# Token norm with tokens on partitions, a small weight piece asked earlier, and a first row in four blocks

## The chip, the cores and the metric

The kernel runs on one core of a Trainium2 chip. A core has five engines that run side by side, each through its own list of instructions: TensorE (PE, matrix products, with its weight loads shown apart as PEld), VectorE (DVE), ScalarE (ACT), GpSimd (POOL) and SyncE (SP, which here only asks for transfers). They wait for one another by semaphores. Data comes from memory through 16 DMA engines. The metric is the device time of one execution in microseconds, lower is better.

## The reference

One block of a diffusion backbone, for 512 latent tokens of 2048 channels and 256 context tokens. What matters for this case is the head of it: each token is divided by the root of the mean of its squares, multiplied by a per-channel gain, and shifted; gain and shift come from a product of the conditioning vectors with a weight matrix (the modulation).

```
shift, scale, gate = split(silu(c) @ w_ada + b_ada, 3)
shift_c, scale_c, gate_c = split(silu(c_ctx) @ w_ada + b_ada, 3)
rms(v) = v * rsqrt(mean(v * v, axis=-1) + EPS) * norm_g
h  = rms(x)   * (1 + scale)   + shift       # 512 x 2048
hc = rms(ctx) * (1 + scale_c) + shift_c
p  = h @ w_in                               # q, k, v, gates, Fourier branch: 2048 x 9216
...                                         # attention, Fourier mixing, projections
out = rms_final(x + gate * y)
```

## The kernel before

All large products are made in three terms of a high and a low part (`mm3`, lines 339 to 341: high by high, high by low, low by high), with both parts of f32r type. A weight piece of 128 x 1024 that arrives as f32 is split by `split_from`: ACT copies it to the high part (line 181), DVE subtracts that for the low part (line 182).

The channels lie on partitions: `xt` holds x transposed, 16 rows (`kb`, the kernel's word for a block of 128 channels) of 128 partitions by 512 tokens. The first stage, before the kernel's long steady part, does this:

- SP asks for x in nine transfers (line 477, tile `xt`), then for the weights of the first rows' modulation (tile `wa`, `in_w_ss`; the first matrix, `kb` = 0, in one half and two quarters, which are its second half) and for pieces of the input projection (tile `wr`, `in_w_start`, line 217). All these go through one queue in the order of the program.
- `token_norms` squares x (ACT, for two rows DVE), adds the squares of two rows (DVE, line 546) and sums them over the 128 partitions by products with ones on PE (line 548), eight groups, one after each pair. Between groups PE gets a product that nobody reads (`warm`, line 528) to keep it busy. Then ACT takes the root (line 553), DVE the reciprocal (line 554), and `spread` (line 560) puts the 512 values on all partitions, in a PSUM tile `pc`.
- `matvec(0, 0)` and `matvec(0, 1)` (line 567) multiply the conditioning vectors by the two halves of the first modulation matrix, with `spread` between them in PE's order. `taken` (line 583) copies the result to the tile `ado`, `turned` transposes it (line 588), `factors` makes gain and shift from it (lines 599 to 602).
- The first row: `by_root` (line 614) multiplies x by the reciprocal root from PSUM, `row_hi` (line 618, ACT) applies gain and shift and rounds to the high part, `scaled` and `row_lo` (lines 621 and 625, DVE) make the low part. `start_work` then runs the products of that row with the first pieces: 256 columns (lines 680, 681, 687), then the other 768 (`mm3`).

In this stage PE, ACT and DVE run in the order in which the program was written (`manual_schedule`). PE therefore waits in line: what stands behind a waiting product waits too.

## Time and profile before

| what | us |
|---|---|
| median of 3 runs | 1287.12 (1286.21 to 1287.29) |
| the profiled execution, device time | 1286.97 |
| its span, first to last instruction | 1285.2 |
| PE busy | 1269.6 (99%) |
| PE weight loads busy | 1045.2 (81%) |
| DVE busy | 991.0 (77%) |
| ACT busy | 683.2 (53%) |
| POOL busy | 173.2 (13%) |

The device time holds the span and 1.77 us around it. The busy time of PE is modelled from pipelined products, so its share says that PE has work nearly all the time, not that it runs at its peak. In rows of a timeline, a group of alike instructions is merged to one row with its count; an f32 product that is one instruction in the program's order is two in the trace.

### The profile page before, as it was taken

To read this page: it belongs to the slowest core of one execution; us is meant where nothing else is said; L and a number is where in the kernel's file an instruction comes from. 1 tells how busy PE (TensorE), PEld (TensorE's weight loads), DVE (VectorE), ACT (ScalarE), POOL (GpSimd) and SP (SyncE) were. 2 spreads that over 40 slices of the span, in tenths; PEclk is the share of its full clock that TensorE was granted. 3 is DMA by queue.
4 is the path that set the end of the run, shared out by engine and by line. 5 is a ranking of instruction groups with operands and counts; after the bars stand their busy time and mean duration, and the time that the engine had idled before them with its cause. 6 is when DMAs were issued, how large, how long until landed. Compare 5 with 4: busy or idle time off the path is not lost.

```text
span 1285.2 us, 17638 instructions
## 1 busy us (share of the span) xinstructions
PE 1269.6 (99%) x6562; PEld 1045.2 (81%) x6562; DVE 991.0 (77%) x1305; ACT 683.2 (53%) x1077; POOL 173.2 (13%) x226
## 2 busy tenths in 40 slices
PE   8999999999999999999999999999999999999997
PEld 5677888888888888888888888888888888888886
DVE  5767899889778787748687756778898777787677
ACT  5322765555466564543355445766667646465544
POOL 0000121111102011012021011011100221211310
PEclk9999999999999999999999999999999999999999
DMA  9998798888898998887879897578852989998986
GB/s 378 412 368 344 242 204 254 229 240 239 234 315 209 320 271 254 291 197 188 282 204 288 254 259 234 180 234 250 265 178 67 260 241 258 245 207 222 227 207 179
DMA packets 104343, 319.07 MB, mean 248 GB/s; under 512 B 9889, under 2 KB 32801, under 8 KB 100289
## 3 DMA queue, kind: packets, MB, share of 16 engines
q1 hardware_dynamic: 54336, 195.24, 41.8%
q0 software_dynamic: 27600, 100.29, 37.0%
q10 hardware_dynamic: 22320, 22.42, 5.1%
q8 instruction: 51, 0.84, 0.3%
q14 instruction: 36, 0.29, 0.1%
HBM read 283.30 MB, written 34.61 MB: 247 GB/s over the span
## 4 chain that ended last, share of the span: by engine, by line
PE 82%; DVE 3%; DMA 2%; ACT 2%; issue 1%; SPq 0%; ACTq 0%
PE banks L339 10%; PE banks L340 10%; PE banks L341 10%; PE x L341 9%; PE x L339 9%; PE x L340 9%; PE y L341 8%; PE y L340 8%; PE y L339 8%; PE banks L1551 2%; DMA wr<-in_w_pab 1%; DVE wlo L182 1%; DMA s<-yb_d 1%; PE banks L1665 1%; DVE s L182 0%
## 5 line engine op out<-in xcount | busy, mean ns | idle before, releaser
L181 ACT ACTIVATE whi<-R 128x1024 fp32r<-128x1024 f32 x138 | 145.1, 1058 | 143.7 <-PE banks L341 47.5
L182 DVE TENSOR_TENSOR wlo<-R,whi 128x1024 fp32r<-128x1024 f32 x138 | 167.7, 1221 | 61.2 <-ACT whi L181 60.9
L182 DVE TENSOR_TENSOR wlo<-wr,whi 128x1024 fp32r<-128x1024 f32 (+1 forms) x122 | 147.3, 1213 | 62.7 <-ACT whi L181 62.5
L181 ACT ACTIVATE whi<-wr 128x1024 fp32r<-128x1024 f32 (+1 forms) x122 | 127.4, 1050 | 123.4 <-PE y L341 33.0
L339 PE MATMUL banks<-whi,s 128*128 128x512 f32 (+1 forms) x400 | 157.8, 394 | 0.9 <-ACT ev L1160 0.7
L340 PE MATMUL banks<-wlo,s 128*128 128x512 f32 (+1 forms) x400 | 155.9, 390 | 0.0
L341 PE MATMUL banks<-whi,s 128*128 128x512 f32 (+1 forms) x400 | 155.8, 389 | 0.0
L339 PE MATMUL x<-whi,s 128*128 128x512 f32 x352 | 137.1, 390 | 0.0
L341 PE MATMUL x<-whi,s 128*128 128x512 f32 x352 | 137.0, 389 | 0.0
L340 PE MATMUL x<-wlo,s 128*128 128x512 f32 x352 | 136.9, 389 | 0.0
L292 POOL DMA_DIRECT2D R<-in_w_g x68 | 59.5, 874 | 484.7 <-DVE wlo L182 290.2
L340 PE MATMUL y<-wlo,s 128*128 128x512 f32 x316 | 123.0, 389 | 0.1
L339 PE MATMUL y<-whi,s 128*128 128x512 f32 x316 | 122.9, 389 | 0.0
L341 PE MATMUL y<-whi,s 128*128 128x512 f32 x316 | 122.8, 389 | 0.0
L181 ACT ACTIVATE s<-wr 128x512 fp32r<-128x512 f32 (+2 forms) x93 | 60.8, 677 | 66.0 <-DMA wr<-cf_d 24.4
L182 DVE TENSOR_TENSOR s<-wr,s 128x512 fp32r<-128x512 f32 (+2 forms) x93 | 66.7, 749 | 31.8 <-ACT s L181 30.9
L339 PEld LDWEIGHTS banks<-whi,s 128*128 128x128 f32 x400 | 75.2, 188 | 16.6 <-ACT ev L1160 1.1
L341 PEld LDWEIGHTS banks<-whi,s 128*128 128x128 f32 x400 | 75.2, 188 | 15.3
L340 PEld LDWEIGHTS banks<-wlo,s 128*128 128x128 f32 x400 | 75.2, 188 | 13.9 <-DVE wlo L182 0.2
L340 PEld LDWEIGHTS x<-wlo,s 128*128 128x128 f32 x352 | 66.1, 188 | 13.8
L341 PEld LDWEIGHTS x<-whi,s 128*128 128x128 f32 x352 | 66.1, 188 | 13.7
L339 PEld LDWEIGHTS x<-whi,s 128*128 128x128 f32 x352 | 66.1, 188 | 13.6
(333 smaller groups left out, 2794.0 us busy)
## 6 DMA issues: line engine op xcount, KB each, us to landing
wr<-in_w_g SPq DMA_DIRECT2D x124, 512.0 KB, 5.6
R<-in_w_g POOLq DMA_DIRECT2D x68, 512.0 KB, 7.4
wa<-in_w_ss SPq DMA_DIRECT2D x31, 1024.0 KB, 9.5
R<-in_w_g SPq DMA_DIRECT2D x32, 512.0 KB, 5.8
wr<-in_w_gate SPq DMA_DIRECT2D x32, 512.0 KB, 5.1
wr<-in_w_o SPq DMA_DIRECT2D x24, 512.0 KB, 7.1
R<-in_w_o POOLq DMA_DIRECT2D x24, 512.0 KB, 8.9
wr<-in_w_pab SPq DMA_DIRECT2D x20, 512.0 KB, 6.1
```

The lines of the kernel that those rows point to most:

```text
L181: first = nc.scalar.activation(hi, src, ACT.Copy)
L182: return first, nc.vector.tensor_tensor(lo, src, hi.bitcast(F32), op=ALU.subtract)
L292: chained[:] = [nc.gpsimd.dma_start(chain[e.pc], e.nxt, accum_op=ALU.add)]
L339: nc.tensor.matmul(o, ah, bh, start=start, stop=False, skip_group_check=cont)
L340: nc.tensor.matmul(o, ah, bl, start=False, stop=False, skip_group_check=cont)
L341: nc.tensor.matmul(o, al, bh, start=False, stop=stop, skip_group_check=cont)
L1551: nc.tensor.transpose(tp[:, k * P : (k + 1) * P], p[:, k * P : (k + 1) * P], ident)
L1665: last_turn[0] = nc.tensor.transpose(tp[:, k // 2, 256 * (k % 2) + P * t : 256 * (k % 2) + P * t + P], m[:, t, k * P : k * P + P], ident)
```

## The change

Three parts, all in the first stage.

1. The sums of squares. Before, ones (32 columns wide) were PE's weights and the squares streamed through, so that each group of 128 tokens had its sums along the free axis, in a strip of 32 partitions of its own. Now the squares of 128 tokens are the weights and one column of ones streams, so that the sums stand with tokens on partitions, in four columns. The last pair of rows isn't added by DVE any more; both rows go to PE. Root and reciprocal work on 128 x 4 instead of 128 x 128. `spread` uses a column of the reciprocals, repeated 128 times, as weights and the identity as the streaming side. The selection table `pick`, and its memsets on POOL, are gone. One `warm` product instead of three follows the first transpose.
2. The small piece `wr` of 128 x 256 is asked for ahead of the last quarter of the first modulation matrix instead of behind it.
3. `row_hi` and `row_lo` of the first row go in four blocks of 128 tokens. And `by_root(0)` stands ahead of the copy of the spread roots to SBUF (`rx`), on which it does not depend.

```
@@ wada_load @@
             for k in (0, 4) if (kb, h) == (0, 1) else (0,):
                 n = 4 if (kb, h) == (0, 1) else 8
+                if (kb, h, k) == (0, 1, 4):
+                    load_start()
                 ask(nc.sync, r[-1][:, k : k + n, :], w_ss[kb, :, 8 * h + k : 8 * h + k + n, :])
...
     wada = {0: wada_load(0)}
-    for _ in range(2):
-        load_start()
+    load_start()
@@ token_norms @@
-        t = hm_tile([P, 2, T], F32, name=uid("nm"))
-        pick, r = t[:, 0, :].rearrange("p (t c) -> p t c", t=4), t[:, 1, :P]
-        nc.gpsimd.memset(pick, 0.0)
-        for t in range(4):
-            nc.gpsimd.memset(pick[32 * t : 32 * t + 1, t, :], 1.0)
-        acc = bank2()
+        r = hm_tile([P, 2, T], F32, name=uid("nm"))[:, 0, :4]
+        acc = bank2()[:, :4]
...
-            nc.vector.tensor_tensor(a, a, b, op=ALU.add)
-            for t in range(4):
-                nc.tensor.matmul(acc[32 * t : 32 * t + 32, :P], ones[:, :32], a[:, t * P : t * P + P],
-                                 start=q == 0, stop=q == KK - 2)
+            if q < KK - 2:
+                nc.vector.tensor_tensor(a, a, b, op=ALU.add)
+            for v in (a,) if q < KK - 2 else (a, b):
+                for t in range(4):
+                    nc.tensor.matmul(acc[:, t : t + 1], v[:, t * P : t * P + P], ones[:, :1], start=q == 0 and t == 0,
+                                     stop=q == KK - 2 and v is b and t == 3, skip_group_check=True)
...
-        nc.scalar.activation(r, acc[:, :P], ACT.Sqrt, bias=eps_t[:, 0:1], scale=1.0 / D)
+        nc.scalar.activation(r, acc, ACT.Sqrt, bias=eps_t[:, 0:1], scale=1.0 / D)
         nc.vector.reciprocal(r, r)
@@ spread @@
-            nc.tensor.matmul(acc[:, t * P : t * P + P], pick[:, t, :], r, start=True, stop=True)
+            nc.tensor.matmul(acc[:, t * P : t * P + P], r[:, t : t + 1].broadcast_to([P, P]), ident, start=True, stop=True)
@@ turned @@
         if kb == 0:
-            warm(3, o)
+            warm(1, o)
@@ row_hi, row_lo @@
+    tokens_of = lambda kb: [slice(P * t, P * t + P) for t in range(4)] if kb == 0 else [slice(0, T)]
-        nc.scalar.activation(hhi[kb], y_of[kb], ACT.Identity, bias=shift[:, kb, 0:1], scale=gain[:, kb, 0:1])
+        for c in tokens_of(kb):
+            nc.scalar.activation(hhi[kb][:, c], y_of[kb][:, c], ACT.Identity, bias=shift[:, kb, 0:1], scale=gain[:, kb, 0:1])
-        v = xt[:, kb, :]
-        nc.vector.scalar_tensor_tensor(hlo[kb], v, shift[:, kb, 0:1], hhi[kb].bitcast(F32),
-                                       op0=ALU.add, op1=ALU.subtract)
+        for c in tokens_of(kb):
+            nc.vector.scalar_tensor_tensor(hlo[kb][:, c], xt[:, kb, c], shift[:, kb, 0:1], hhi[kb][:, c].bitcast(F32),
+                                           op0=ALU.add, op1=ALU.subtract)
@@ the order of the first stage @@
-            nc.scalar.copy(rx, rx0[0])
             by_root(0)
+            nc.scalar.copy(rx, rx0[0])
             split_next()
             taken(0)
```

PE's list at the last group of the norm sums and the first modulation product, before (`pd` is the PSUM tile of the sums and then of the modulation, `s` the squares and the reciprocals, `wa` the modulation weights; the streaming side is named first, the weights behind the comma):

```order
L548 MATMUL pd_166<-s_221,ones 32x128 x4
L548 MATMUL pd_166<-s_229,ones 32x128 x4
L567 MATMUL pd_239<-wa_122,c_137 32x256 x8
L560 MATMUL pc_248<-s_160 128x128 x4
L567 MATMUL pd_239<-wa_124,c_137 32x256 x8
```

and after:

```order
L547 MATMUL pd_161<-ones,s_216 128x1 x4
L547 MATMUL pd_161<-ones,s_224 128x1 x8
L566 MATMUL pd_237<-wa_122,c_137 32x256 x8
L559 MATMUL pc_246<-ident,s_160 128x128 x4
L566 MATMUL pd_237<-wa_124,c_137 32x256 x8
```

The places are the same; the sums have ones and squares exchanged, and the last group is eight products instead of four.

ACT's list from the root to the split of the 768-column piece, with what each waits for, before:

```order
L553 ACTIVATE s_160<-pd_166,eps_t 128x128 [waits DVE_49,PE_49]
L785 COPY rx<-pc_248 128x512 [waits PE_49]
L181 ACTIVATE whi_265<-wr_127 128x256 [waits DMAHW5_49]
L583 COPY ado_269<-pd_239 128x256 [waits PE_49]
L618 ACTIVATE s_286<-S_67,shift,gain 128x512 [waits DVE_49]
L181 ACTIVATE whi_291<-wr_129 128x768 [waits DMAHW6_49]
```

and after:

```order
L552 ACTIVATE s_160<-pd_161,eps_t 128x4 [waits DVE_49,PE_49]
L787 COPY rx<-pc_246 128x512 [waits DVE_49]
L181 ACTIVATE whi_263<-wr_126 128x256 [waits DMAHW4_49]
L582 COPY ado_267<-pd_237 128x256 [waits PE_49]
L619 ACTIVATE s_282<-S_67,shift,gain 128x128 [waits DVE_49]
L619 ACTIVATE s_282<-S_67,shift,gain 128x128 x3
L181 ACTIVATE whi_293<-wr_129 128x768 [waits DMAHW6_49]
```

The copy `rx` waits for DVE now instead of PE, and the row stands as four blocks ahead of the same split.

SP's list between x and the second modulation matrix, before:

```order
L477 DMA wa_122<-in_w_ss 128x2048
L477 DMA wa_124<-in_w_ss 128x1024 x2
L217 DMA wr_127<-in_w_start 128x256
L217 DMA wr_129<-in_w_start 128x768
L477 DMA wa_131<-in_w_ss 128x2048
```

and after:

```order
L477 DMA wa_122<-in_w_ss 128x2048
L477 DMA wa_124<-in_w_ss 128x1024
L217 DMA wr_126<-in_w_start 128x256
L477 DMA wa_124<-in_w_ss 128x1024
L217 DMA wr_129<-in_w_start 128x768
L477 DMA wa_131<-in_w_ss 128x2048
```

The small piece has moved up by one place, past 512 KB.

## The prediction

> **What bounds the kernel now.** I read the page's engine totals first, then the busy time in three stretches, then the start in order of time.

> ```profile
> span 1285.2 us, 17638 instructions
> PE 1269.6 (99%) x6562; PEld 1045.2 (81%) x6562; DVE 991.0 (77%) x1305; ACT 683.2 (53%) x1077; POOL 173.2 (13%) x226
> ```

> ```profile
> core 0: us, PE busy (x) PEld busy (x) DVE busy (x) ACT busy (x) POOL busy (x), PEclk, DMA share, GB/s
> 0.00:24.20 24.20, 19.65 (x154) 12.13 (x154) 13.09 (x29) 14.33 (x24) 1.91 (x11) 1.00 0.94 366
> 24.20:1277.60 1253.40, 1249.87 (x6410) 1033.08 (x6409) 975.27 (x1270) 667.26 (x1050) 171.26 (x215) 1.00 0.84 246
> 1277.60:1285.20 7.60, 0.07 (x1) 0.00 (x0) 2.60 (x7) 1.63 (x3) 0.00 (x0) 0.85 0.67 251
> ```

> From 24.2 us to 1277.6 us the TensorE stands still for only 1253.40 - 1249.87 = 3.5 us. So whatever the change does to the moment at which the steady products begin goes one to one into the end: later stages have almost no slack to give back, and almost no stalls to save. All of the change lies before 24.2 us. That stretch, in order of time (start, duration, engine, line, tiles; in brackets the idle time before and who ended it):

> ```profile
> 1.05 3.48 PEld L528 LDWEIGHTS pc<-ones 128*128 128x128 f32 x16 [1.05 <-DVE eps_t L351]
> 7.00 0.66 PE L548 MATMUL pd<-s,ones 128*32 128x128 f32 x8 [2.17 <-DVE s L546]
> 7.59 1.22 PE L528 MATMUL pc<-s,ones 128*128 128x256 f32 x2
> 8.74 0.66 PE L548 MATMUL pd<-s,ones 128*32 128x128 f32 x8
> ...
> 12.21 0.66 PE L548 MATMUL pd<-s,ones 128*32 128x128 f32 x8
> 13.59 0.43 PE L548 MATMUL pd<-s,ones 128*32 128x128 f32 x8
> 13.94 0.70 PE L528 MATMUL pc<-s,ones 128*128 128x256 f32 x2
> 14.33 0.61 ACT L545 ACTIVATE s<-xt 128x512 f32<-128x512 f32 x1
> 14.57 0.43 PE L548 MATMUL pd<-s,ones 128*32 128x128 f32 x8
> 15.56 0.64 PE L548 MATMUL pd<-s,ones 128*32 128x128 f32 x16
> 16.61 1.07 PE L567 MATMUL pd<-wa,c 128*32 128x256 f32 x16 [0.41 <-DMA wa<-in_w_ss]
> 16.67 0.95 DVE L554 RECIPROCAL s<-s 128x128 f32<-128x128 f32 x1 [1.00 <-ACT s L553]
> 17.74 0.97 PEld L560 LDWEIGHTS pc<-s 128*128 128x128 f32 x8 [0.54 <-issue]
> 18.83 1.07 PE L567 MATMUL pd<-wa,c 128*32 128x256 f32 x16
> 18.93 0.59 ACT L785 COPY rx<-pc 128x512 f32<-128x512 f32 x1 [2.30 <-PE pc L560]
> 19.20 0.22 PEld L567 LDWEIGHTS pd<-wa,c 128*32 128x32 f32 x8 [0.22 <-DMA wa<-in_w_ss]
> 19.51 0.42 ACT L181 ACTIVATE whi<-wr 128x256 fp32r<-128x256 f32 x1
> 19.55 0.69 DVE L614 TENSOR_TENSOR S<-xt,pc 128x512 f32<-128x512 f32 x1 [1.93 <-ACT rx L785]
> 19.96 0.37 ACT L583 COPY ado<-pd 128x256 f32<-128x256 f32 x1
> 20.39 0.44 PE L588 MATMUL pd<-ident,ado 128*128 128x128 f32 x2 [0.49 <-ACT ado L583]
> 21.34 0.22 DVE L602 TENSOR_SCALAR shift<-adr,small 128x2 f32<-128x2 f32 x1
> 21.60 0.81 ACT L618 ACTIVATE s<-S,shift,gain 128x512 fp32r<-128x512 f32 x1 [1.26 <-DVE shift L602]
> 22.32 0.83 ACT L181 ACTIVATE whi<-wr 128x768 fp32r<-128x768 f32 x1
> 22.46 0.39 PE L680 MATMUL pb<-whi,s 128*128 128x256 f32 x1 [0.34 <-ACT s L618]
> 23.18 0.96 DVE L182 TENSOR_TENSOR wlo<-wr,whi 128x768 fp32r<-128x768 f32 x1
> 24.20 0.39 PE L340 MATMUL pb<-wlo,s 128*128 128x256 f32 x1
> ```

> The reader is to see three things. First, the path that sets the start: norm sums until 16.2, the first half of the first modulation product at 16.61 (held by its weights, which land then), the spreading of the roots at 17.74, the second half at 18.83, the ACT copy, the turn at 20.39, shift and gain, the row at 21.60, the first real product at 22.46, and at 24.20 the product that waits for the 768-column split. Second, the norm groups run at two paces: one every 1.74 us at first (7.00, 8.74), one every 0.98 us later (13.59, 14.57). The pace changes between 12.21 and 13.59, and the same product takes 0.66 us before and 0.43 after: the TensorE clock was half until about 13.2 us. Third, at half clock the PE, not the squares, already sets the pace.

> **The change, part by part.** I price against the profiled execution, 1286.97 us (span 1285.2 and 1.77 around it), which lies 0.15 under the median of 1287.12.

> *Norm sums.* Before, `ones[:, :32]` are the weights: four narrow loads per pass, in four column strips that run side by side, and 128 columns stream. Now the squares themselves are the weights: each of the four products of a group loads 128 columns and streams one. The program's x4 is x8 in the trace, since an f32 product goes in two passes; so a group has 8 full loads, and the last pair, no longer added by DVE, has 16. In all 7 x 8 + 16 = 72 full loads, each into the whole array, so none beside another. Their price: the rows at 1.05 and 17.74 and these durations of single loads,

> ```profile
> L528 PEld LDWEIGHTS pc<-ones x16: 286/333/333, 1.0 to 4.2; 128*128 128x128 f32 x16
> L560 PEld LDWEIGHTS pc<-s x8: 186/192/192, 17.7 to 18.5; 128*128 128x128 f32 x8
> ```

> give a step from load to load of (3.48 - 0.33) / 15 = 0.210 us at half clock and (0.97 - 0.19) / 7 = 0.111 at full clock. In these rows a load and a 128-column product overlap, so the step could be the product's; ends are 0.025 (the 32-column loads at 19.20: 0.22 / 8) and 0.333 or 0.19 (no overlap at all). I take 0.210 and 0.111, since these are loads of exactly this width and type. Besides, each of the first six groups keeps its warm-up product: 8.74 - 7.59 = 1.15 us at half clock and 14.57 - 13.94 = 0.63 at full, of which I keep 0.95 and 0.50, because the pause at the switch from column strips to the whole array goes. A group then costs 8 x 0.210 + 0.95 = 2.63 us at half clock (now 1.74) and 8 x 0.111 + 0.50 = 1.39 at full (now 0.98). If the clock rises at the same 13.16 us: 6.16 / 2.63 = 2.34 groups are done by then, 3.66 remain, 3.66 x 1.39 = 5.09, and the last 24 loads take 2.66; the sums end at 20.9 instead of 16.2. The weights of the modulation product lie ready since 16.61, so 20.9 - 16.6 = 4.3 us come onto the path.

> [...]

> *Small operations of the norm.* The last DVE add, most of the 0.95 us reciprocal and part of the root on ACT go, as do five memsets on POOL. All lie now beside the 1.07 us of the first half product, which stands between the sums and the spreading in PE's order: nothing on the path. The same holds if that cover moves, since it moves with the sums.

> *The copy and the first multiplication change places.* Both read the same PSUM tile, and the order of waits makes the second reader wait for the first: before, the multiplication at 19.55 was released by the copy. Now ACT's copy waits for DVE's 0.69 us. Queued behind it on ACT are the small split (0.42) and the copy of the modulation sums (0.37), for which PE's turn waits. Ends: 0 (if the sums' product were later anyway) and 0.69. The copy of the sums started 1.03 us after the rx copy and PE needs about 1.0 us after the spreading, so there is no room: I take 0.6.

> *Small piece ahead of the last quarter.* Its 128 KB pass ahead of the last 512 KB on SP's queue, and everything between 10 and 20 us runs at

> ```profile
> 10.00:20.00 10.00, 9.40 (x98) 4.40 (x96) 5.57 (x9) 5.37 (x11) 0.00 (x0) 1.00 1.04 410
> ```

> 410 GB/s, so the last quarter lands 131 KB / 410 GB/s = 0.32 us later, at about 19.5. With PE late by 4 us both have long landed: 0. If PE is not late, 0.2 to 0.3 us of loss at the wait of 19.20.

> *First row in four blocks.* Prices from the nearest rows of 128 columns with a column operand:

> ```profile
> L1545 ACT ACTIVATE s<-s,gain 128x128 f32<-128x128 f32 x48 | 18.8, 400 | 4.6 <-DVE gain L1544 4.6
> L1346 DVE SCALAR_TENSOR_TENSOR qr<-qr,shift 128x128 f32<-128x128 f32 x16 | 5.2, 345 | 0.0
> ```

> Four of 0.40, each overlapping the one before by some 0.1 (22.32 starts before 21.60 + 0.81), are 1.3 us instead of 0.81. The first product can start 0.4 us earlier, but it gains nothing that lasts: the 768-column split is queued behind the four blocks on ACT, starts 0.5 us later, and so does its low part on DVE, for which PE waits at 24.20. Ends: 0 and 0.8 (no overlap). I take 0.5.

> Sum: 4.3 + 0.6 + 0 + 0.5 = 5.4, and 1286.97 + 5.4 = 1292.4 us. If the clock rises one window of 3.41 us earlier, the same working ends the sums at 19.3 (1290.8), one later at 22.5 (1294.0). That is this case's own range.

> **The rivals.** *B, the clock stays half.* What woke the clock?

> ```profile
> 6.33:9.75 3.42, 2.75 (x19) 1.33 (x20) 2.25 (x4) 2.93 (x5) 0.00 (x0) 1.00 1.02 419
> 9.75:13.16 3.41, 3.41 (x21) 1.35 (x21) 2.74 (x5) 2.18 (x4) 0.00 (x0) 1.00 1.05 410
> ```

> The stretch before the change of pace was the first with PE busy throughout. With loads in a row PE's row would be full too. But if only streamed columns count, a half-clock group streams 2 x 256 columns in 2.63 us, about a third of the time, against nearly three quarters before, and nothing wakes the clock until the modulation products. Then the six groups end at 7.0 + 6 x 2.63 = 22.8, the last 24 loads at 27.8, 11.2 us late, and the 3.3 us from 16.61 to 19.9 run slow as well (1 to 3 us more): with the 1.1 of the other parts 13 to 15 us, 1300 to 1302. [...]

> *C, not slower: the loads hide.* If full loads go as fast as the narrow ones, the sums still end before the weights land at 16.61, and what remains is at most the 1.1 us of the two small parts: 1287.0 to 1288.1. It decides at a load cost: from 7.00 to 16.61 are 9.6 us, the six warm-up products take about 2.3 x 0.95 + 3.7 x 0.50 = 4.0, and 5.6 us for 72 loads are 0.078 each. Against it stand 0.111 and 0.210.

> *D, faster by over 0.2%.* 2.6 us would have to go between the landing of the last quarter at 19.2 and the row's product at 22.46, a stretch of 3.3 us of which 2.1 lie after the turn and are not shortened. Hardly possible.

> **How the numbers follow.** A measurement of this kernel tells 0.2% (2.6 us) from no change. Chances: A, the sum above, 0.47; B 0.31; C 0.19; D 0.03. So slower 0.78, same 0.19, faster 0.03, and the forecast is A's 1292.4. For 8 in 10 the range takes A whole, nearly all of B and the upper end of C: 1287.4 to 1301.5. A's own range is 1290.8 to 1294.0.

> **What the new profile would show.** Right: the norm sums' loads 0.21 and then 0.11 us apart, no idle PE between the groups, the last of them ending near 21 us, the product of 16.61 starting there with no wait for DMA, the rx copy released by DVE, the product of 24.20 near 29.6. B would show loads at 0.33 us each and warm-up products at 0.63 right up to 27 us. C would show the groups keeping pace with the squares, whose last one ends at 14.9. I am wrong if a full load takes under 0.08 us, or if something after 24.2 us moves.

## The result, and the profile after

The kernel became slower: 1299.87 us (median of 5 runs, 1299.62 to 1300.58) against 1286.32 (median of 5 runs, 1286.21 to 1287.29), a ratio of 1.0103 with a 95% interval of 1.0089 to 1.0117. The profiled execution took 1299.63 us, a span of 1297.9 and 1.73 around it.

The page's totals, and the busy time in two stretches (start and end, length, then busy time and count for each engine):

```profile
span 1297.9 us, 17644 instructions
PE 1283.2 (99%) x6566; PEld 1062.1 (82%) x6566; DVE 989.9 (76%) x1307; ACT 682.8 (53%) x1080; POOL 171.7 (13%) x221
```

```profile
core 0: us, PE busy (x) PEld busy (x) DVE busy (x) ACT busy (x) POOL busy (x), PEclk, DMA share, GB/s
0.00:37.40 37.40, 32.59 (x157) 27.79 (x157) 12.21 (x30) 14.96 (x27) 0.68 (x6) 0.66 0.84 318
37.40:1290.30 1252.90, 1250.53 (x6411) 1034.34 (x6410) 975.11 (x1271) 666.19 (x1050) 171.02 (x215) 1.00 0.83 244
```

The long stretch is as long as before (1252.90 against 1253.40 us) and PE stands still in it for 2.4 us instead of 3.5. All of the loss lies ahead of it: the start takes 37.4 us instead of 24.2, and its mean granted clock is 0.66.

The start in order of time (start, duration, engine, line, tiles; in brackets the idle time before and who ended it):

```profile
7.21 0.97 PEld L547 LDWEIGHTS pd<-ones,s 128*128 128x128 f32 x8 [2.69 <-DVE s L544]
8.48 1.93 PEld L547 LDWEIGHTS pd<-ones,s 128*128 128x128 f32 x8
10.93 2.04 PEld L547 LDWEIGHTS pd<-ones,s 128*128 128x128 f32 x8
13.49 2.04 PEld L547 LDWEIGHTS pd<-ones,s 128*128 128x128 f32 x8
...
21.17 5.46 PEld L547 LDWEIGHTS pd<-ones,s 128*128 128x128 f32 x24
...
26.64 1.93 PE L566 MATMUL pd<-wa,c 128*32 128x256 f32 x16
28.51 2.08 PE L559 MATMUL pc<-ident,s 128*128 128x128 f32 x8
30.51 1.94 PE L566 MATMUL pd<-wa,c 128*32 128x256 f32 x16
30.62 0.69 DVE L614 TENSOR_TENSOR S<-xt,pc 128x512 f32<-128x512 f32 x1 [3.40 <-PE pc L559]
31.34 0.58 ACT L787 COPY rx<-pc 128x512 f32<-128x512 f32 x1 [4.33 <-DVE S L614]
32.52 0.37 ACT L582 COPY ado<-pd 128x256 f32<-128x256 f32 x1 [0.27 <-PE pd L566]
32.94 0.44 PE L587 MATMUL pd<-ident,ado 128*128 128x128 f32 x2 [0.49 <-ACT ado L582]
34.15 1.65 ACT L619 ACTIVATE s<-S,shift,gain 128x128 fp32r<-128x128 f32 x4 [1.26 <-DVE shift L601]
35.70 0.83 ACT L181 ACTIVATE whi<-wr 128x768 fp32r<-128x768 f32 x1
37.58 0.58 PE L340 MATMUL pb<-wlo,s 128*128 128x256 f32 x1
```

From the third on the norm groups run at one pace to the end, one every 2.56 us (10.93, 13.49); the first takes 1.27. Before, the pace changed at about 13 us. The modulation and the spreading, too, still run at half clock: 1.93, 2.08 and 1.94 us, which were 1.07, 1.13 and 1.07. The product that waits for the 768-column split starts 13.38 us later (37.58 against 24.20). By stations:

| from, to | before | after | difference |
|---|---|---|---|
| start to the first half modulation product | 16.61 | 26.64 | +10.03 |
| from there to the turn of the modulation | 3.78 | 6.30 | +2.52 |
| from there to the product of 24.20 | 3.81 | 4.64 | +0.83 |

The same columns as in the stretches above, for four stretches cut where the granted clock changed:

```profile
5.07:8.48 3.41, 1.26 (x10) 1.19 (x10) 1.39 (x2) 2.95 (x6) 0.00 (x0) 1.00 1.02 405
8.48:32.38 23.90, 23.90 (x116) 20.19 (x114) 5.64 (x10) 6.26 (x12) 0.00 (x0) 0.50 0.87 338
32.38:35.79 3.41, 2.04 (x14) 1.36 (x10) 2.35 (x8) 2.01 (x6) 0.00 (x0) 1.00 0.79 257
35.79:39.20 3.41, 3.41 (x16) 3.19 (x15) 1.92 (x4) 0.74 (x2) 0.00 (x0) 0.50 0.63 257
```

The clock was full for one piece of 3.41 us, just after the eight warm-up products at the program's beginning had ended (at 4.82), then half for 23.9 us in which PE's row is full without a gap, then full, half once more, and full from 39.20 on.

### The profile page after: what moved, and what is told of

Read it like the earlier page. It is cut to its first block, busy times and chain, and to the rows that moved or that the text cites. A ratio compares the mean times of both kernels' runs of the same rounds, so it can differ in the third digit from the quotient of the medians.

```text
span 1297.9 us, 17644 instructions
## 1 busy us (share of the span) xinstructions
PE 1283.2 (99%) x6566; PEld 1062.1 (82%) x6566; DVE 989.9 (76%) x1307; ACT 682.8 (53%) x1080; POOL 171.7 (13%) x221
## 4 chain that ended last, share of the span: by engine, by line
PE 94%; DMA 2%; DVE 1%; ACT 1%; issue 1%; POOL 0%; SPq 0%; ACTq 0%; DVEq 0%; POOLq 0%
PE banks L339 10%; PE banks L340 10%; PE banks L341 10%; PE x L341 9%; PE x L339 9%; PE x L340 9%; PE y L341 8%; PE y L340 8%; PE y L339 8%; PE banks L1552 2%; PE pd L566 2%; PE pc L339 1%; PE pb L339 1%; PE pc L341 1%; PE pc L340 1%; PE pb L340 1%
## 5 line engine op out<-in xcount | busy, mean ns | idle before, releaser
L181 ACT ACTIVATE whi<-R 128x1024 fp32r<-128x1024 f32 x138 | 145.1, 1058 | 139.3 <-PE banks L341 49.2
L182 DVE TENSOR_TENSOR wlo<-R,whi 128x1024 fp32r<-128x1024 f32 x138 | 167.8, 1222 | 60.2 <-ACT whi L181 59.9
L182 DVE TENSOR_TENSOR wlo<-wr,whi 128x1024 fp32r<-128x1024 f32 (+1 forms) x122 | 147.6, 1214 | 64.5 <-ACT whi L181 64.3
L181 ACT ACTIVATE whi<-wr 128x1024 fp32r<-128x1024 f32 (+1 forms) x122 | 127.4, 1050 | 118.3 <-PE y L341 36.3
L340 PE MATMUL banks<-wlo,s 128*128 128x512 f32 (+1 forms) x400 | 156.1, 390 | 0.0
L340 PE MATMUL x<-wlo,s 128*128 128x512 f32 x352 | 137.1, 390 | 0.0
L340 PE MATMUL y<-wlo,s 128*128 128x512 f32 x316 | 123.2, 390 | 0.3 <-DVE wlo L182 0.3
L181 ACT ACTIVATE s<-wr 128x512 fp32r<-128x512 f32 (+2 forms) x93 | 60.7, 676 | 67.3 <-DMA wr<-cf_d 23.5
L182 DVE TENSOR_TENSOR s<-wr,s 128x512 fp32r<-128x512 f32 (+2 forms) x93 | 66.9, 751 | 34.1 <-ACT s L181 33.2
L340 PEld LDWEIGHTS banks<-wlo,s 128*128 128x128 f32 x400 | 75.3, 188 | 13.9 <-DVE wlo L182 0.3
L340 PEld LDWEIGHTS x<-wlo,s 128*128 128x128 f32 x352 | 66.1, 188 | 13.7
L339 PEld LDWEIGHTS x<-whi,s 128*128 128x128 f32 x352 | 66.1, 188 | 13.5
```

Source lines behind the costliest of these rows:

```text
L181: first = nc.scalar.activation(hi, src, ACT.Copy)
L182: return first, nc.vector.tensor_tensor(lo, src, hi.bitcast(F32), op=ALU.subtract)
L339: nc.tensor.matmul(o, ah, bh, start=start, stop=False, skip_group_check=cont)
L340: nc.tensor.matmul(o, ah, bl, start=False, stop=False, skip_group_check=cont)
```

## The experiments

Here "before" and "after" name the two kernels. Two theories: **loads** ("Rival L" in the expectations), that the price is that of 72 full weight loads and the small parts, the clock aside; and **clock** ("Theory S"), that a stream of loads with one streamed column does not wake the clock, and that most of the time is lost to half speed. Shares of streaming below are estimates: 128 columns take 0.21 us at half clock (the step of the row at 1.05 in the prediction), 256 columns 0.42, an f32 product two passes. In after a group takes 2.56 us, of which 8 loads of 0.213 are 1.70; the other 0.86 go to the warm-up product's two passes of 256 columns, which agrees.

**Norm sums alone** (e1_sums_only): before, with the first part of the change and nothing else of it.

```
 before, with from after:
+    token_norms, spread          # squares as weights, one column of ones streamed
 and as before: warm(3, o); rx copied ahead of by_root(0); row in one piece; small piece behind the quarter
```

> The kernel before with part 1 alone (sums with tokens on partitions, last pair not added by DVE, spread by repeated weights); order of ACT and DVE, asks, three warm-up products and whole first row as before. Theory S (the clock gate counts streamed columns, and loads with one column leave it at half clock until the modulation products): sums end near 26.6 us as in the changed kernel, 1298 to 1299.5 us, and the clock does not drop a second time in the first row. Rival L (most of the loss is the loads' own time and the small parts, the clock only follows): sums end earlier than 24 us, 1292 to 1296.

Measured: 1299.6 us (1298.69 to 1301.04), ratio 1.0102 (1.0088 to 1.0115). That is all of the difference, as far as the intervals tell, and just above the range expected. The sums end at 27.41 us, and the clock rises once, at 30.42, and does not fall again in the start.

**The rest alone** (e2_rest_only): after, with the norm sums and the spreading of before.

```
 after, with from before:
+    token_norms, spread          # ones as weights, squares streamed
```

> The changed kernel with the norm sums and the spreading of before: small piece early, copy behind the multiplication, first row in four blocks, one warm-up product after the turn. Theory S: sums end near 16.2 us at a clock that has risen by 13 us; the prices of the prediction give 0.6 for the copy, 0.5 for the blocks, up to 0.3 for the piece, so 1286.9 to 1287.8; if the clock drops after the thin first row (as it does in the changed kernel at 35.8 us) another 1.5 us. Rival L: these parts carry several us, 1289 to 1292.

Measured: 1288.68 us (1287.27 to 1290.24), ratio 1.0014 (1.0005 to 1.0023), 0.9 us more than the upper end expected. Its rows of the timeline:

```profile
21.14 0.44 PE L589 MATMUL pd<-ident,ado 128*128 128x128 f32 x2 [0.97 <-ACT ado L584]
25.78 0.39 PE L340 MATMUL pb<-wlo,s 128*128 128x256 f32 x1 [0.61 <-DVE wlo L182]
```

The turn is 0.75 us later than before (20.39), and the product of 24.20 comes 1.58 later. The other parts cost something, but not 13 us.

**The same loads, more streamed columns.** In three kernels each product of the sums streams several equal columns of ones and writes as many equal columns, of which the root reads one. Number, order and width of the weight loads stay those of after. 128 columns:

```
-        acc = bank2()[:, :4]
+        acc = bank2()[:, : 4 * 128]
-  nc.tensor.matmul(acc[:, t : t + 1], v[...], ones[:, :1], ...)
+  nc.tensor.matmul(acc[:, 128 * t : 128 * t + 128], v[...], ones[:, :128], ...)
-  nc.scalar.activation(r, acc, ACT.Sqrt, ...)
+  nc.scalar.activation(r, acc.rearrange("p (t c) -> p t c", t=4)[:, :, 0], ACT.Sqrt, ...)
```

> The changed kernel, but each product of the norm sums streams 128 equal columns of ones instead of one (the sum is read from the first of each 128). Same 72 loads, same order, same additions. Theory S: at a given clock a group hardly gets longer, since the load takes as long as 128 columns (0.21 us at half clock, 0.11 at full), but streaming is now near 90% of the time and the clock rises within two windows of 3.4 us: loads 0.11 apart by 14 us, sums end at 18 to 21, time 1290 to 1293. Rival L or a clock that is low for another reason: sums still end at 26 us or later and the time stays at 1299.5 to 1302.

Measured: 1291.6 us (1291.0 to 1293.53), ratio 1.0041 (1.0027 to 1.0055). With 128 times the streamed columns the kernel is 8.3 us faster than after. From its timeline, and its stretches on both sides of the clock's rise:

```profile
6.93 2.07 PE L547 MATMUL pd<-ones,s 128*128 128x128 f32 x8 [2.11 <-DVE s L544]
9.65 1.30 PE L547 MATMUL pd<-ones,s 128*128 128x128 f32 x8
11.22 1.05 PE L547 MATMUL pd<-ones,s 128*128 128x128 f32 x8
12.55 1.05 PE L547 MATMUL pd<-ones,s 128*128 128x128 f32 x8
...
16.52 2.84 PE L547 MATMUL pd<-ones,s 128*128 128x128 f32 x24
19.29 1.07 PE L566 MATMUL pd<-wa,c 128*32 128x256 f32 x16
```

```profile
6.75:10.16 3.41, 3.23 (x13) 3.06 (x14) 2.13 (x5) 2.51 (x6) 0.00 (x0) 1.00 1.03 422
10.16:13.57 3.41, 3.41 (x28) 3.31 (x28) 2.65 (x4) 2.61 (x5) 0.00 (x0) 1.00 1.06 412
```

The group falls from 2.72 us (6.93 to 9.65) to 1.33 (11.22 to 12.55): the clock rose at 10.16. (2.72 is the time of a first group at half clock: with 64 columns, below, it lasts from 7.09 to 9.81.) The 1.00 in the first of the two stretches is filled in, since the trace has no clock record before its first change; the durations tell the half clock there. Loads filled 3.06 of the 3.41 us ahead of the rise, no more than in a stretch of after in which nothing rose:

```profile
11.89:15.30 3.41, 3.41 (x16) 3.23 (x16) 2.35 (x4) 2.59 (x5) 0.00 (x0) 0.50 1.06 420
```

What differs is what streams: an estimated 2.52 of a group's 2.72 us (93%), against 0.84 of 2.56 (33%) in after.

64 and 32 columns, with the same lines:

> As e3 with 64 streamed columns per product. Theory S: a group at half clock takes 2.56 us as in the changed kernel and streams 8 x 0.107 + 0.854 = 1.71 of it, 67%. Windows seen so far with about 59% streamed did not raise the clock, one with about 73% did; so this one lies between: if 67% is enough, the clock rises by 14 us and the time is 1290.5 to 1293.5, if not 1299 to 1301.

> As e3 with 32 streamed columns per product: streamed share (8 x 0.053 + 0.854) / 2.56 = 50%. Theory S: below the 59% that did not raise the clock, so it stays at half clock, sums end near 27 us, 1299 to 1301. A theory in which any product wider than one column counts as busy in full gives 1290.5 to 1293.5.

Measured: 1302.07 us with 64 (1299.34 to 1304.38, ratio 1.0118, 1.0102 to 1.0135) and 1302.49 with 32 (1301.7 to 1302.94, ratio 1.0122, 1.0107 to 1.0137). In both the clock is half from the second group on at the latest, to 33.42 and 32.01 us, and groups keep 2.56 us; the share of streaming is 1.68 of 2.56 (66%) and 1.26 of 2.56 (49%). So by these estimates the point from which the clock rises in these kernels lies between 66% and the 72% of before (1.26 of 1.74), if the share of streaming is what counts. These are means over a group; a piece of 3.41 us does not hold whole groups, so the two ends are rough. Both times lie above the 1299 to 1301 expected, some 2 us above after. Of that the start shows 1.1 and 0.4 us (the product of 24.20 comes at 38.70 and 37.99, in after at 37.58); the rest is not explained.

**Warm-up products, taken away.** From after and from before the product between the groups is left out; nothing reads its result.

```
-            if q < KK - 4:
-                warm(1, two[:, 0, :256])
```

> The changed kernel without the six warm-up products between the groups of sums. Theory S: they stream too little to raise the clock and only take time, 0.85 us each at half clock; 72 loads of 0.213 us are 15.4 us, the sums end at 22.5 instead of 26.7 and the time falls by 4 to 5 us to 1295 to 1296. If the warm-up products do keep the clock from something worse, or if loads alone counted as busy, the time would not fall by this: 1299 to 1301, or under 1292.

> The kernel before without its six warm-up products. Theory S: narrow loads cost nothing, so the groups keep pace with the squares and the sums end by 16.5 us, but they stream only 0.43 us in 1.29, a third; the clock stays at half through the modulation products, and what follows 16.6 us runs slow until the first full window: 1288.5 to 1291.5, 2 to 5 us over the kernel before. That is what the clock costs without the loads. If the clock had nothing to do with what is streamed: 1286 to 1287.5.

Measured: after without them 1294.71 us (1294.09 to 1296.01, ratio 1.0064, 1.0048 to 1.0081), before without them 1288.59 (1287.45 to 1292.01, ratio 1.0017, 1.0008 to 1.0027). The first is a little under the 1295 to 1296 expected, the second at the lower end of its range. The timeline of the first, and its stretch at half clock, up to the end of the sums and as a whole:

```profile
8.39 13.62 PE L547 MATMUL pd<-ones,s 128*128 128x1 f32 x64 [0.23 <-DVE s L544]
21.94 1.93 PE L564 MATMUL pd<-wa,c 128*32 128x256 f32 x16
32.46 0.38 PE L340 MATMUL pb<-wlo,s 128*128 128x256 f32 x1 [0.61 <-DVE wlo L182]
```

```profile
8.63:21.94 13.31, 13.31 (x65) 13.29 (x64) 4.67 (x7) 4.94 (x9) 0.00 (x0) 0.50 1.03 414
8.63:25.69 17.06, 17.06 (x88) 15.65 (x87) 4.85 (x8) 5.20 (x10) 0.00 (x0) 0.50 1.02 412
```

Here are 64 full loads by themselves: 13.62 / 64 = 0.213 us each, so the price at half clock was right. From 8.63 to 21.94 PE's row is full, and its loads' row too (13.29 of 13.31 us), and the clock stays at 0.50 until two thirds of the modulation and spreading have passed. In after the six warm-up products therefore cost PE time, 0.86 us each at half clock, and wake nothing: with them and without, the clock rose only behind the sums, at 32.38 and at 25.69 us. In before they pay some 2 us (1.0 to 3.5 by the interval of the ratio): there the clock rose at 13.16 us with them and at 20.09 without. The second's rows, the first of them at half clock:

```profile
16.61 1.94 PE L565 MATMUL pd<-wa,c 128*32 128x256 f32 x16 [0.24 <-DMA wa<-in_w_ss]
25.69 0.39 PE L340 MATMUL pb<-wlo,s 128*128 128x256 f32 x1
```

The sums end in time for 16.61 even so, and the loss is 1.49 us at the product of 24.20: what follows 16.61 runs slowly until the clock rises at 20.09.

**Three warm-up products after the turn** (e4_warm3), to see whether the second fall of the clock costs:

```
         if kb == 0:
-            warm(1, o)
+            warm(3, o)
```

> The changed kernel with three warm-up products after the turn, as before, instead of one. Theory S: the second fall of the clock, from 35.8 to 39.2 us, goes away because the window before it streams more; 1298 to 1299, that is 0.7 to 1.7 us faster than the changed kernel. If the fall comes from the four thin blocks alone, no difference: 1299.6 to 1300.2.

Measured: 1299.04 us (1297.99 to 1301.53), ratio 1.0099 (1.0085 to 1.0113), not to be told from after. In its profile the second fall is gone, and the product of 24.20 starts at 37.52 instead of 37.58, so that fall costs little; whether it costs the 0.8 us between the medians is open. That the two products keep the clock up is not shown either: with 32 columns (from 32.01 us) and without the products between the groups (from 25.69) only one stands after the turn, and the clock does not fall.

**The small parts, each alone in before.**

```
e9_swap_only     by_root(0) ahead of nc.scalar.copy(rx, rx0[0])
e10_blocks_only  row_hi and row_lo of row 0 in four blocks of 128 tokens
e11_piece_only   load_start() ahead of the last quarter's ask
```

> The kernel before with the first multiplication ahead of the copy of the roots, nothing else. My price: ACT's chain to the turn starts 0.6 us later; in e2 the way from the spreading to the turn was 3.10 us instead of 2.62, so the turn comes 0.5 to 0.7 us later: 1286.7 to 1287.7 against some 1286.6 for the kernel before. Rival: the copy is off the path, no shift of the turn.

> The kernel before with the first row in four blocks, nothing else. In e2 the way from the turn to the product that waits for the 768-column split was 4.64 us instead of 3.81, so 0.8 us later here too (my price was 0.5): 1287.0 to 1288.0. If the two warm-up products that are kept here matter for the clock after the turn, e2's larger loss does not show here.

> The kernel before with the small piece asked ahead of the last quarter of the first modulation matrix, nothing else. My price: the last quarter lands 0.32 us later and the second half product waits for it, 0.2 to 0.3 us more there: 1286.3 to 1287.3, not to be told from the kernel before by its time but by the start of the turn in the trace (20.6 to 20.7 instead of 20.39). If the earlier split saves more than that on ACT, the turn comes at or before 20.39.

Measured: 1286.68, 1287.81 and 1286.91 us, ratios 1.0 (0.999 to 1.0009), 1.0004 (0.9995 to 1.0013) and 1.0001 (0.9992 to 1.001). None is told from no change by its time; the timelines show what each does, one fence for each kernel:

```profile
19.66 0.58 ACT L786 COPY rx<-pc 128x512 f32<-128x512 f32 x1 [3.02 <-DVE S L614]
20.88 0.44 PE L588 MATMUL pd<-ident,ado 128*128 128x128 f32 x2 [0.97 <-ACT ado L583]
24.69 0.39 PE L340 MATMUL pb<-wlo,s 128*128 128x256 f32 x1
```

```profile
21.56 1.65 ACT L620 ACTIVATE s<-S,shift,gain 128x128 fp32r<-128x128 f32 x4 [1.26 <-DVE shift L602]
24.99 0.39 PE L340 MATMUL pb<-wlo,s 128*128 128x256 f32 x1 [0.61 <-DVE wlo L182]
```

```profile
19.54 0.16 PEld L568 LDWEIGHTS pd<-wa,c 128*32 128x32 f32 x8 [0.60 <-DMA wa<-in_w_ss]
24.48 0.39 PE L340 MATMUL pb<-wlo,s 128*128 128x256 f32 x1
```

The product of 24.20 comes 0.49, 0.79 and 0.28 us later: 1.56 together, against the 1.58 of all three in one kernel (e2_rest_only, which also has one warm-up product instead of three).

## Why the prediction was right or wrong

The direction was right, but the forecast of 1292.4 was 7.5 us short: 5.4 us of loss were forecast and 13.5 measured. The time lies inside the range only because the range took in most of rival B. B is what happened; the working gave it 1300 to 1302 and a chance of 0.31.

**The step that failed** is "If the clock rises at the same 13.16 us". It took the clock as given, from the profile of a kernel in which it rose at 13.16, and moved work under it that streams less (by the estimates above 33% of a group instead of 72%). The clock rose at 32.38 us, after the sums, instead of at 13.16. (With the sums of before, 13.16 is one execution's: the rise lies at 10.53, 10.68, 12.92 and 14.53 in e9_swap_only, e10_blocks_only, e11_piece_only and e2_rest_only.) The price of that step is the difference between after and the kernel with 128 streamed columns, 8.3 us of the 13.5; the other 5.3 are the loads and the small parts. That kernel is case A made real: its clock rose at 10.16 us, 3.0 earlier than before's and near the 10.53 and 10.68 just named, and its sums ended at 19.3 us, where the working said 19.3 and 1290.8 for a rise one window earlier; it took 1291.6. (The start of before, with its one change of the clock, does not show that window of 3.41 us; after's changes at 5.07 and 8.48, and at 32.38, 35.79 and 39.20, have that distance.) That the sums agree to 0.1 us is in part luck, since the groups differ a little from their prices (next paragraph).

**Norm sums.** The load steps were right: 0.213 us at half clock (predicted 0.210), and at full clock (0.97 - 0.19) / 7 = 0.111 in the first group of after. The groups took 2.56 us (predicted 2.63) at half clock and, with 128 streamed columns, 1.33 (1.39) at full; the warm-up product's part was 0.86 us at half clock, where 0.95 was taken. The pause at the switch from strips to the whole array is in the trace of before as 0.38 us without a load ahead of the warm-up product's loads at half clock (7.58, 9.32) and 0.20 at full (13.94); in after these start at 10.29, before the group's last load ends at 10.41. The last of the sums ended at 26.6 us, where rival B said 27.8: one group ran mostly in the early full piece (1.27 us), the others were 0.07 to 0.18 us shorter, and the last 24 loads took 5.47 us instead of 5.04. On the path: +10.03 instead of 4.3.

B rested on "if only streamed columns count", which no row of before shows. For weight loads e7_after_nowarm has the row: 13.29 us of them in 13.31 at a clock of 0.50.

**B's signs** were loads of 0.33 us each and warm-up products at 0.63. Both came, as the durations of single instructions (smallest, median and largest, in ns):

```profile
L547 PEld LDWEIGHTS pd<-ones,s x72: 186/334/338, 7.2 to 26.3; 128*128 128x128 f32 x72
L529 PE MATMUL pc<-s,ones x12: 463/635/775, 8.1 to 21.2; 128*128 128x256 f32 x12
```

But loads overlap and follow at 0.213 us, so 0.33 is no price. The surer sign was the pace of the groups.

**From the first half product to the turn**: predicted 0.6, for the copy behind the multiplication. Measured 2.52, and for another reason: three stretches of PE at half clock, +0.74 (16.61 to 17.74, now 26.64 to 28.51), +0.91 (to 18.83, now 30.51) and +0.88 (to the copy of the sums, 19.96, now 32.52). The order of copy and multiplication itself costs nothing in after: the row at 32.52 was released by PE, with ACT idle for 0.27 us before it. At full clock and alone (e9_swap_only) it moves the turn by 0.49 us, close to the step's 0.6.

**Small piece**: 0 in after, as said. Alone, the last quarter's load starts 0.34 us later (19.54 for 19.20; predicted 0.32) and the product of 24.20 0.28 (predicted 0.2 to 0.3).

**Row in four blocks**: predicted 0.5, from four blocks of 0.40 us with 0.1 of overlap at each joint. The four take 1.65 us instead of 0.81. They do overlap, by 0.09 us at each joint (4 x 0.48 - 3 x 0.09 = 1.65); it was the block that was priced too low, from a row with one column operand; these have two, which may be the reason but is not tested:

```profile
L619 ACT ACTIVATE s<-S,shift,gain x4: 477/478/493, 34.2 to 35.3; 128x128 fp32r<-128x128 f32 x4
```

The product of 24.20 comes 0.79 us later alone and 0.83 after the turn in after, the upper of the two ends given.

**C and D** are out: with the loads' price confirmed, the sums come after the landing of the weights at 16.61, even with the clock full from 10.16 us on (19.3 in e3_wide128). That nothing behind the start would give back was nearly right: of 13.38 us the span shows 12.7.

## What to carry to other kernels

When products change which operand is loaded and which streams, work out the share of time in which columns stream, at half clock, and not only the sum of the durations: here a full row of PE, and of its loads (13.29 of 13.31 us), left the clock at 0.50. Exchanging the operands of a thin product saved a little vector work here (a DVE add of 0.69 us, and 0.18 us for the reciprocal instead of 0.95) and paid one full load per 128 columns, at 0.213 us instead of 0.111 while the clock was half. And whether a warm-up product is worth its time is to be measured in the kernel at hand: the same six gained some 2 us in one kernel, whose clock rose at 13.16 us with them and at 20.09 without, and lost 5 in the other, whose clock rose only behind the sums, at 32.38 us with them and at 25.69 without.

## What the runs showed of the hardware

```profile
31.89:35.30 3.41, 2.89 (x20) 1.81 (x12) 2.06 (x7) 2.15 (x7) 0.00 (x0) 1.00 0.89 298
```

```profile
32.01:35.42 3.41, 1.87 (x18) 0.89 (x10) 1.84 (x7) 2.02 (x6) 0.00 (x0) 1.00 0.87 305
```

- Two readers of one PSUM tile, on ACT and DVE, stood one behind the other in either order: in before the multiplication at 19.55 was released by the copy, in e9_swap_only the copy at 19.66 by the multiplication, which put the turn 0.49 us later.
